# Moving a decoder layer's parameter and weight loads between DMA queues, and a subtraction between engines

## The chip, the cores and the metric

The kernel runs on one core of a Trainium2 chip. TensorE multiplies, VectorE and ScalarE do the arithmetic around it, GpSimd does small element-wise work, and SP issues most of the DMAs. The metric is the device time of one execution in microseconds, given as the median of several runs. A profiled execution leaves a trace, whose span runs from the first to the last instruction.

## What is computed

One layer of a hybrid decoder, for a prompt of 2048 positions and for 8 sample sequences of 4 positions:

```python
xn = _rmsnorm(x, g_attn_norm)
q, k, v, u = split(xn @ w_in)                    # q, k normed per head; 8 heads of 64
branches = [_dilated_branch(q, k, v, r) for r in (1, 4, 16)]   # 128 strided keys each, ALiBi
attn = _merge_branches(branches)                 # weights: softmax over the branches' log-sum-exp
h = x + concat([attn, pool_mixer(u)]) @ w_out
y = h + conv_ffn(_rmsnorm(h, g_ffn_norm))        # up-projection, conv of width 3, SiLU gate, down-projection
```

Each float32 product is made as three products of rounded halves (hi x hi, hi x lo, lo x hi), so every weight and every activation is split first: ScalarE rounds it (line 112), another engine subtracts the rounded part (line 113).

## The kernel before

The work has three stages, each with its own pools in SBUF. The first projects the 16 tiles of 128 rows of the prompt, tile by tile; queries and keys go to DRAM turned and split (`spill_qk`), values as rows (`finish_v`). What belongs to the end of a tile is put off by a number of bursts (`later.after`), and a burst comes at the end of each projection. The last projections are those of the values of tiles 14 and 15, and around them lie the loads for head 0 (`load_qk`, `load_v`): columns 0 to 1535 ahead of them, the last 512 columns behind them, all on SP's queue.

The second stage is attention. It has 192 items, 24 for each of the 8 heads; an item is two blocks of 128 queries of one head and one pattern p (0, 1, 2 for dilation 1, 4, 16). `advance(i)` does the scores of item i, the transposes of item i - 2 and the value products of item i - 3, and copies spread queries on GpSimd for item i + 6 (`spread_next`). From item 8 on the order on every engine is written out by hand (`manual_schedule`, lines 721 to 742); outside it the compiler's scheduler picks the order. Into this loop, at lines 730 to 739, are put:

- the parameter rows of the later stage: `param_load(j)` on SP's queue every 8 items from item 24, turned 13 items later by `param_turn`. Rows and output weights share two buffers (tag `row`);
- the first half (512 columns) of the output weights, one row tile every 5 items from item 150: allocation, load on SP's queue and split, all in one item (lines 735 to 739, tile `rawo`).

The values of the next heads come on SP's queue too (`next_v`, 4 to 8 DMAs each), as do the queries and keys of the next head (`load_head`, 6 DMAs) and the stores of finished outputs (`store_o`).

The third stage merges the three patterns' outputs, multiplies by the output weights (`out_part`, line 817) and runs the feed-forward part. At its start, lines 840 to 846 merge the first four row tiles (`merge`, lines 775 to 797), and load and split the second half of the output weights with `load_rows`: four pairs of row tiles, two of them after the merge of tile 0 and two after that of tile 1, with the subtraction of the split on GpSimd. The loads have three buffers (tag `raw`).

Of the kernel before, what the change touches and what calls it, by code (L numbers as in the profile page):

```python
# [9 lines left out]
F32 = mybir.dt.float32  # L10
# [7 lines left out]
P = 128  # L18
S = 2048
DM = 1024  # L20
KT = DM // P
H = 8
DH = 64
# [8 lines left out]
CH = 512  # L32
# [6 lines left out]
RUN = 4  # L39
# [3 lines left out]
def f32(ap):  # L43
    return ap.bitcast(F32)
# [3 lines left out]
def kernel(ctx, tc, ins, cst, outs):  # L48
    nc = tc.nc
# [8 lines left out]
    w_in0, w_out0, w_up0, w_down0 = w_in[0], w_out[0], w_up[0], w_down[0]  # L58
# [18 lines left out]
    qT_hi = dram.tile([AW, S], F32, name="qT_hi")  # L77
    qT_lo = dram.tile([AW, S], F32, name="qT_lo")
    kT_hi = dram.tile([AW, S], F32, name="kT_hi")
# [31 lines left out]
    def split(hi, lo, src, eng=None):  # L111
        nc.scalar.copy(hi, src)  # L112
        (eng or nc.vector).tensor_tensor(out=lo, in0=src, in1=f32(hi), op=ALU.subtract)  # L113
# [41 lines left out]
    def qk_tile():  # L155
        return pq.tile([P, 3, S], F32R, tag="QK", name="QK", bufs=2)

    def load_qk(h, qk, cols):
        rows = slice(h * DH, (h + 1) * DH)
        Q, KH, KL = (qk[:, i, cols] for i in range(3))  # L160
        nc.sync.dma_start(f32(Q[0:DH]), qT_hi[rows, cols])
        nc.sync.dma_start(f32(Q[DH:P]), qT_lo[rows, cols])
        for half in range(2):
            hr = slice(half * DH, (half + 1) * DH)
            nc.sync.dma_start(f32(KH[hr]), kT_hi[rows, cols])
            nc.sync.dma_start(f32(KL[hr]), kT_lo[rows, cols])

    def bias_table(h):
        tab = pq.tile([P, 3, 2 * P], F32, tag="tab", name="tab", bufs=2)
# [7 lines left out]
        nc.gpsimd.memset(t[:, :, P + 1:P + 2], 1.0)  # L177
        return t

    def load_v(hp, p, t, lo, hi):  # L180

        vs = v_s[:, hp * P:(hp + 1) * P]
        d = t[:, :, 1:P + 1]
        if p == 0:
            nc.sync.dma_start(d, vs.rearrange("(n i) f -> i n f", i=P)[:, lo:hi])
        else:
            r = DILS[p]
            n = min(r, hi - lo)
            for j in range(lo, hi, n):
                J, c = divmod(j, r)  # L190
                src = vs[J * P * r:(J + 1) * P * r].rearrange("(m c i) f -> i m c f", c=r, i=RUN)[:, :, c:c + n]
                for i in range(RUN):
                    nc.sync.dma_start(d[i::RUN, j - lo:j - lo + n, :], src[i])

    rows_of = {}
    stv = state_ffn_conv[0].rearrange("b r c -> (b r) c")
# [1 line left out]
    def param_load(j):  # L198
        n = 2 * NF if j < 4 else 2 * SB
        row = rows_of[j] = p2.tile([2 * NF, 4 * P], F32, tag="row", name="row", bufs=2)  # L200
        if j < 4:
            src = conv_b if j == 3 else conv_w[0, j:j + 1]
            nc.sync.dma_start(row[:, 0:P], src.rearrange("l (c p) -> (l c) p", p=P))
        else:
            nc.sync.dma_start(row[:n], stv[:, (j - 4) * 4 * P:(j - 3) * 4 * P])

    def param_turn(j):
        row = rows_of.pop(j)
# [38 lines left out]

    pair_v, pair_o, heads, spread = {}, {}, {}, {}

    def next_v(hp, p, half):  # L250
        t = value_tile(p2, "V")
        load_v(hp, p, t, 8 * half, 8 * half + 8)
        for b in range(8):
            pair_v[hp, p, 8 * half + b] = t[:, b, :]

# [114 lines left out]
    with tc.tile_pool(name="p1", bufs=1) as p1:  # L370
# [125 lines left out]
        def finish_qk(t, j, ps):  # L496
            rows = P if t >= 0 else NSMP
            a = p1.tile([rows, AW], F32, tag="t", name="a", bufs=4)
            a3 = a.rearrange("p (h d) -> p h d", d=DH)
            nc.scalar.activation(a, ps, AF.Square)  # L500
            ssq = p1.tile([rows, H], F32, tag="ssq", name="ssq", bufs=2)
            nc.vector.tensor_reduce(out=ssq, in_=a3, axis=AX.X, op=ALU.add)
            r = rms_scale(p1, ssq, H, DH)
            nc.vector.tensor_tensor(out=a3, in0=ps.rearrange("p (h d) -> p h d", d=DH),
                                    in1=r[:, :, None].to_broadcast([rows, H, DH]), op=ALU.mult)
            nc.vector.tensor_tensor(out=a, in0=a, in1=g_b[j][:rows], op=ALU.mult)
            if t < 0:
                if j == 0:
                    nc.sync.dma_start(q_smp, a)
                else:  # L510
                    nc.sync.dma_start(nks, a)
                    nc.sync.dma_start(k_smp[:, 3:, :], a)
                return
            if j == 1:
                (nc.gpsimd if t == S // P - 1 else nc.sync).dma_start(nk[t * P:(t + 1) * P, :], a)
            later.after(2, lambda: spill_qk(t, j, a))

        def spill_qk(t, j, a):
            tp = tp4(a)
            for i, dst in enumerate(((qT_hi, qT_lo), (kT_hi, kT_lo))[j]):  # L520
                s = p1.tile([P, 4, P], F32R, tag="qkh", name="qkh", bufs=3)
                d, src = s, tp
                if j == 1:
                    d = s.rearrange("p a (g c i) -> p (a g) c i", c=RES, i=RUN)
                    src = tp.rearrange("p a (g i c) -> p (a g) c i", c=RES, i=RUN)
                if i == 0:
                    hi = d
                    nc.scalar.copy(hi, src)
                else:
                    nc.vector.tensor_tensor(out=d, in0=src, in1=f32(hi), op=ALU.subtract)  # L530
                nc.sync.dma_start(dst.rearrange("(a p) t -> p a t", p=P)[:, :, t * P:(t + 1) * P], f32(s))
# [145 lines left out]
        for half in range(2):  # L677
            pair_o[0, half] = O_first[:, 8 * half:8 * half + 8]
        later.flush()
        load_qk(0, qk, slice(3 * CH, S))  # L680
        load_v(0, 0, v_first[:, 12:16], 12, 16)
        for b in range(16):
            pair_v[0, 0, b] = v_first[:, b, :]
        for i in range(AHEAD):
# [9 lines left out]
    def h_tile(k):  # L694

        return ph.tile([P, 2, TM], F32R, tag=f"h{k}", name="h", bufs=1)
# [13 lines left out]

    with tc.tile_pool(name="p2", bufs=1, reuse_waits="tile") as p2:
        wo0 = [h_tile(k) for k in range(KT)]
        for half in range(2):
            for p in (2, 1):
                next_v(0, p, half)
        nc.vector.memset(stT[:, :, 2 * SB:], 0.0)
        for i in range(AHEAD, AHEAD + SPREAD):
            spread_next(i)
        NEXT_V = {(1, 14): (2, 0), (1, 17): (0, 0), (1, 21): (1, 0), (1, 23): (0, 1), (0, 1): (2, 1), (0, 3): (1, 1)}

        with tc.manual_schedule():
            for i in range(AHEAD, len(items) + 3):
                if i < len(items):
                    h, li = divmod(i, NI)
                    if (i == AHEAD or h and li == 4) and h + 1 < H:
                        load_head(h + 1)

                    if (h % 2, li) in NEXT_V and 0 < h < H - (h % 2):
                        next_v((h + 1) // 2, *NEXT_V[h % 2, li])
                    j, r = divmod(i - NI, 8)  # L730
                    if r == 0 and 0 <= j < 15:
                        param_load(j)
                    if r == 5 and 0 < j < 16:
                        param_turn(j - 1)
                    if i >= 150 and i % 5 == 0 and i < 190:
                        k = ((i - 150) // 5 + 4) % KT
                        raw = p2.tile([P, CH], F32, tag="row", name="rawo", bufs=2)
                        nc.sync.dma_start(raw, wov[:, k, 0:CH])
                        split(wo0[k][:, 0, 0:CH], wo0[k][:, 1, 0:CH], raw)
                    if (h, li) == (7, 0):  # L740
                        mBs[0] = load_pool(0)
                advance(i)
# [3 lines left out]
    with tc.tile_pool(name="p4", bufs=1, reuse_waits="tile") as p4:  # L746
# [11 lines left out]
        def load_rows(view, k0, half, eng=None):  # L758
            raw = raw_tile().rearrange("p (a k) f -> p a (k f)", a=2)
            n = min(2, view.shape[0] // P - k0)  # L760
            nc.sync.dma_start(raw[:, :n], view[k0 * P:(k0 + n) * P, half * CH:(half + 1) * CH]
                              .rearrange("(k p) f -> p k f", p=P))
            w = w_tile().rearrange("p a (b k) f -> p a b (k f)", b=2)
            split(w[:, 0, :n], w[:, 1, :n], raw[:, :n], eng)
            return [w[:, :, i, :] for i in range(n)]
# [4 lines left out]
        def merge_load(t):  # L770
            Om = p4.tile([P, 3, 4, OW], F32, tag="ex", name="om", bufs=2)
            nc.sync.dma_start(Om, o_s.rearrange("(n t) h f -> t n h f", n=3)[t * P:(t + 1) * P])
            return Om
# [63 lines left out]
        NT = S // P  # L837
        res, mAs, ats = {}, {}, {}
        groups = [tuple(range(4))] + [(t, t + 1) for t in range(4, NT, 2)]
        pre = {t: merge_load(t) for t in range(2)}  # L840
        for t in groups[0]:
            ats[t] = merge(pre.pop(t) if t in pre else merge_load(t))
            for k in (((4, 6), (0, 2), (), ()))[t]:
                for j, w in enumerate(load_rows(w_out0, k, 1, nc.gpsimd)):
                    wo[1][k + j] = [w[:, b, :] for b in range(2)]
            res[t] = load_res(t)
        g_ffn_b = p4.tile([P, DM], F32, name="g_ffn_b")
        nc.sync.dma_start(g_ffn_b, g_ffn_norm.to_broadcast([P, DM]))
# [445 lines left out]
```

## Time and profile before

| | |
|---|---|
| median of 3 runs | 2561.21 us (2559.82 to 2563.23) |
| profiled execution | 2559.28 us |
| its span | 2557.5 us |
| TensorE busy | 2486.2 us (97%) |
| VectorE busy | 1725.1 us (67%) |
| ScalarE busy | 1079.1 us (42%) |
| GpSimd busy | 186.6 us (7%) |
| DMA moved | 393.58 MB, 154 GB/s in the mean |

How to read it: a busy TensorE is one with instructions in flight, and its share is an average over stages. The page also cuts the span into 40 slices of 64 us, with the busy tenths of each engine and the TensorE clock that was granted. The rows below are from views of single stretches. PE is TensorE, PEld its weight loads, DVE VectorE, ACT ScalarE, POOL GpSimd, SP the engine that issues DMAs (SPq and POOLq are the issuing queues). L112 is line 112 of the kernel; `out<-in` are the names of the tiles.

### The profile page before, as it was taken

What the parts mean: (1) busy time and instruction counts of PE and PEld (TensorE: products, weight loads), DVE (VectorE), ACT (ScalarE), POOL (GpSimd) and SP (SyncE); (2) the same over time, 40 slices, a digit from 0 to 9 for tenths busy, and PEclk for the clock granted to TensorE, in tenths of its full rate; (3) what the DMA queues carried; (4) which work ended last, traced back from release to release, by engine and by line L of the source; (5) the groups of instructions that cost most, each with busy time, mean ns of one, the idle gap of its engine ahead of it and who ended that gap; (6) DMA issues with size and microseconds to landing.
All of it is one profiled execution on the core that took longest, in us unless ns stands there. A gap on an engine that the chain in (4) does not pass through costs nothing.

```text
span 2557.5 us, 36059 instructions
## 1 busy us (share of the span) xinstructions
PE 2486.2 (97%) x13310; PEld 2119.1 (83%) x13310; DVE 1725.1 (67%) x3819; ACT 1079.1 (42%) x2021; POOL 186.6 (7%) x246
## 2 busy tenths in 40 slices
PE   7999999999968999999999999999999999999999
PEld 5888887999867888788888888888888889999997
DVE  7445344566545785888987789887887666666655
ACT  6333332566544222544333454443444444445442
POOL 1111111333311100000000000000000000000000
PEclk9999999899978999999999999999999999999999
DMA  6333334767644997855558434447443436222321
GB/s 221 106 123 107 128 95 130 183 167 184 155 109 136 312 303 251 258 177 184 170 160 257 124 116 150 127 132 252 144 140 98 137 113 226 84 84 85 92 76 61
DMA packets 412875, 393.58 MB, mean 154 GB/s; under 512 B 16347, under 2 KB 319543, under 8 KB 410012
## 3 DMA queue, kind: packets, MB, share of 16 engines
q1 hardware_dynamic: 412476, 390.48, 50.2%
q8 instruction: 105, 1.72, 0.3%
q0 software_dynamic: 224, 0.80, 0.1%
q14 instruction: 70, 0.57, 0.1%
HBM read 305.70 MB, written 85.52 MB: 153 GB/s over the span
## 4 chain that ended last, share of the span: by engine, by line
PE 66%; DMA 1%; DVE 1%; issue 0%; ACT 0%; SPq 0%; POOL 0%; DVEq 0%; POOLq 0%; ACTq 0%
PE pu L1038 38%; PE pd L1214 19%; PE po L817 5%; PE pd L1208 1%; PE tp L122 0%; DMA raw<-in_w_out_dram 0%; PE Op L325 0%; DMA raw<-in_w_up_dram 0%; PE sacc L990 0%; PE sacc L989 0%; PE po L1071 0%; DVE at L796 0%; PE tpa L802 0%; DMA h_s<-ya 0%; PE tpf L1106 0%
## 5 line engine op out<-in xcount | busy, mean ns | idle before, releaser
L1038 PE MATMUL pu<-h,w 128*128 128x512 f32 (+1 forms) x5232 | 990.6, 350 | 2.1 <-ACT w L112 1.6
L1038 PEld LDWEIGHTS pu<-h,w 128*128 128x128 f32 x5232 | 851.1, 188 | 133.4 <-ACT w L112 2.0
L1214 PE MATMUL pd<-w,act 128*128 128x512 f32 x2112 | 490.2, 392 | 0.0
L1214 PEld LDWEIGHTS pd<-w,act 128*128 128x128 f32 x2112 | 396.6, 188 | 88.1
L112 ACT CAST w<-raw 128x1024 fp32r<-128x1024 f32 (+1 forms) x282 | 287.2, 1027 | 295.6 <-PE pd L1214 171.1
L113 DVE TENSOR_TENSOR w<-raw,w 128x1024 fp32r<-128x1024 f32 (+1 forms) x278 | 328.8, 1186 | 27.1 <-ACT w L112 27.0
L471 PE MATMUL ps<-W_hi,xh 128*128 128x512 f32 x1024 | 332.8, 398 | 1.0 <-ACT xh L112 1.0
L1182 DVE SCALAR_TENSOR_TENSOR cv<-ex,cw,cv 128x512 f32<-128x512 f32 x352 | 262.4, 745 | 29.6 <-ACT cv L1174 27.3
L1172 ACT COPY ex<-pu 128x512 f32<-128x512 f32 (+1 forms) x220 | 110.3, 501 | 346.7 <-PE pu L1038 346.6
L471 PEld LDWEIGHTS ps<-W_hi,xh 128*128 128x128 f32 x1024 | 192.9, 189 | 43.1 <-ACT xh L112 1.5
L296 ACT ACTIVATE Pt<-T,st 128x256 f32<-128x256 f32 (+1 forms) x384 | 157.0, 456 | 130.0 <-DVE st L294 128.0
L325 PE MATMUL Op<-V,PTs 128*128 128x65 f32 x1200 | 168.7, 281 | 37.0 <-ACT PTs L308 28.5
L294 DVE CUSTOM_DVE_ANT_0 T<-Sp,tab 128x256 f32<-128x256 f32 (+1 forms) x384 | 125.0, 364 | 118.0 <-PE Sp L289 78.7
L471 PE MATMUL ps<-W_lo,xh 128*128 128x512 f32 x512 | 202.8, 396 | 0.0
L1216 DVE TENSOR_TENSOR ya<-ya,pd 128x512 f32<-128x512 f32 x192 | 131.0, 684 | 101.6 <-PE pd L1214 101.1
L325 PEld LDWEIGHTS Op<-V,PTs 128*128 128x128 f32 x1200 | 159.7, 203 | 44.8 <-ACT PTs L308 35.3
L95 POOL TENSOR_TENSOR rs<-ms,mhalf 128x8 f32<-128x8 f32 (+3 forms) x68 | 76.5, 1126 | 1585.1 <-DVE stT L1175 1049.5
L1174 ACT ACTIVATE cv<-pu,cw 128x512 f32<-128x512 f32 (+3 forms) x264 | 166.3, 650 | 0.0
L112 ACT CAST act<-cv 128x512 fp32r<-128x512 f32 x88 | 54.6, 620 | 162.5 <-DVE cv L1191 156.3
L471 PEld LDWEIGHTS ps<-W_lo,xh 128*128 128x128 f32 x512 | 96.8, 189 | 19.8
L1175 DVE COPY stT<-ex 128x2 f32<-128x2 f32 x176 | 28.8, 163 | 117.0 <-ACT ex L1172 117.0
L303 PE MATMUL tp<-ident,Pt 128*128 128x128 f32 x600 | 103.8, 286 | 0.0
(225 smaller groups left out, 2739.9 us busy)
## 6 DMA issues: line engine op xcount, KB each, us to landing
raw<-in_w_up_dram SPq DMA_DIRECT2D x176, 512.0 KB
raw<-in_w_down_dram SPq DMA_DIRECT2D x80, 512.0 KB
hn_s<-w SPq DMA_DIRECT2D x16, 1024.0 KB
h<-hn_s SPq DMA_DIRECT2D x32, 512.0 KB
far<-in_cache_k_dram SPq DMA_DIRECT2D x64, 256.0 KB
far<-in_cache_v_dram SPq DMA_DIRECT2D x64, 256.0 KB
om<-o_s SPq DMA_DIRECT2D x16, 792.0 KB
raw<-in_w_in_dram SPq DMA_DIRECT2D x16, 512.0 KB
```

The source lines that it names most:

```text
L112: nc.scalar.copy(hi, src)
L113: (eng or nc.vector).tensor_tensor(out=lo, in0=src, in1=f32(hi), op=ALU.subtract)
L294: nc.vector.tensor_tensor_reduce(out=T[:, :w], in0=Sp[:, s, :w], in1=tab[:, p, 2 * P - w:], op0=ALU.add, op1=ALU.min, scale=1.0, scalar=3e ...
L296: nc.scalar.activation(Pt[:, s, :w], T[:, :w], AF.Exp, bias=st[:, i8:i8 + 1], scale=-1.0)
L325: nc.tensor.matmul(Op[:, i4, :], PT[:, j, :], pair_v[hp, p, b][:, v0:v0 + DH + 1], start=n == 0, stop=n == m - 1)
L471: nc.tensor.matmul(ps, xh[:, a, k, :], (W_hi, W_lo)[b][j, k // 2][:, k % 2, :], start=n == 0, stop=n == 3 * KT - 1)
L817: nc.tensor.matmul(ps, lhs, wo[half][k + 4 * (1 - part)][b], start=part == 0 and k == 0 and i == 0, stop=part == 1 and k == 3 and i == 2)
L1038: nc.tensor.matmul(ps[:, :n], w[:, a, k, :], hs[k][:, b, c0:c0 + n], start=i == 0, stop=i == 3 * KT - 1)
L1174: nc.scalar.activation(d, s, AF.Identity, bias=cw[:, 3, ct:ct + 1], scale=cw[:, 2, ct:ct + 1])
L1182: nc.vector.scalar_tensor_tensor(out=d, in0=e[j], scalar=cw[:, j, ct:ct + 1], in1=d, op0=ALU.mult, op1=ALU.add)
L1214: nc.tensor.matmul(ps, act[0][:, a, k, tau * P:(tau + 1) * P], wd[k][:, b, :], start=k == 0 and j == 0, stop=k == n - 1 and j == 2)
L1216: nc.vector.tensor_tensor(out=ysl, in0=ysl, in1=ps, op=ALU.add)
```

## The change

The diff does five things. The last 512 columns of head 0's queries and keys, and the values with them, are loaded by ScalarE's queue. The first eight value loads of pattern 1 and all 15 parameter rows are loaded by GpSimd's queue. The spill of tile 15's keys is put off by one burst and not two. The first half of the output weights is loaded by GpSimd's queue every 4 items from item 150 on, and the split of a tile stands seven items behind its load. The second half's subtractions go to VectorE, and the loads of its pairs 4 and 6 are asked for ahead of the first merge, those of pairs 0 and 2 behind the merges of tiles 1 and 2.

```diff
-    def load_qk(h, qk, cols):
+    def load_qk(h, qk, cols, eng=None):
+        eng = eng or nc.sync
...
-        nc.sync.dma_start(f32(Q[0:DH]), qT_hi[rows, cols])
+        eng.dma_start(f32(Q[0:DH]), qT_hi[rows, cols])
...
-            nc.sync.dma_start(row[:, 0:P], src.rearrange("l (c p) -> (l c) p", p=P))
+            nc.gpsimd.dma_start(row[:, 0:P], src.rearrange("l (c p) -> (l c) p", p=P))
...
-            later.after(2, lambda: spill_qk(t, j, a))
+            later.after(1 if (t, j) == (S // P - 1, 1) else 2, lambda: spill_qk(t, j, a))
...
-        load_qk(0, qk, slice(3 * CH, S))
-        load_v(0, 0, v_first[:, 12:16], 12, 16)
+        load_qk(0, qk, slice(3 * CH, S), nc.scalar)
+        load_v(0, 0, v_first[:, 12:16], 12, 16, nc.scalar)
...
+        raws = {}
         for half in range(2):
             for p in (2, 1):
-                next_v(0, p, half)
+                next_v(0, p, half, nc.gpsimd if (p, half) == (1, 0) else None)
...
-                    if i >= 150 and i % 5 == 0 and i < 190:
-                        k = ((i - 150) // 5 + 4) % KT
-                        raw = p2.tile([P, CH], F32, tag="row", name="rawo", bufs=2)
-                        nc.sync.dma_start(raw, wov[:, k, 0:CH])
-                        split(wo0[k][:, 0, 0:CH], wo0[k][:, 1, 0:CH], raw)
+                    k, r = divmod(i - 150, 4)
+                    if r == 0 and 0 <= k < KT:
+                        raws[k] = p2.tile([P, CH], F32, tag="row", name="rawo", bufs=2)
+                        nc.gpsimd.dma_start(raws[k], wov[:, (k + 4) % KT, 0:CH])
+                    if r == 3 and 0 < k <= KT:
+                        w = wo0[(k + 3) % KT]
+                        split(w[:, 0, 0:CH], w[:, 1, 0:CH], raws.pop(k - 1))
...
+        def load_second(k):
+            for j, w in enumerate(load_rows(w_out0, k, 1)):
+                wo[1][k + j] = [w[:, b, :] for b in range(2)]
+
         pre = {t: merge_load(t) for t in range(2)}
+        load_second(4)
+        load_second(6)
         for t in groups[0]:
             ats[t] = merge(pre.pop(t) if t in pre else merge_load(t))
-            for k in (((4, 6), (0, 2), (), ()))[t]:
-                for j, w in enumerate(load_rows(w_out0, k, 1, nc.gpsimd)):
-                    wo[1][k + j] = [w[:, b, :] for b in range(2)]
+            if t in (1, 2):
+                load_second(2 * t - 2)
             res[t] = load_res(t)
```

## Rows read from the trace of the kernel before

**Rows 1.** Windows, us: stretch, busy and (instructions) by engine, clock, DMA share, GB/s.
```profile
500.00:690.00 190.00, 186.13 (x1609) 179.82 (x1609) 123.92 (x571) 121.43 (x323) 55.64 (x103) 1.00 0.69 165
699.50:812.30 112.80, 79.74 (x581) 77.33 (x579) 50.46 (x211) 49.26 (x125) 13.09 (x22) 0.77 0.35 94
699.50:724.00 24.50, 0.41 (x4) 0.17 (x2) 2.23 (x10) 1.78 (x5) 0.10 (x1) 0.57 0.77 174
724.00:736.60 12.60, 12.54 (x59) 12.55 (x60) 5.04 (x21) 5.46 (x16) 1.46 (x5) 0.50 0.04 14
788.80:795.00 6.20, 0.61 (x6) 0.37 (x4) 2.00 (x7) 1.48 (x3) 0.00 (x0) 0.71 0.57 161
795.00:802.00 7.00, 6.96 (x34) 6.96 (x35) 2.58 (x12) 2.71 (x8) 0.00 (x0) 0.52 0.14 41
```

**Rows 2.** Waits from 690 us on: waiter, releaser, us in total, times, longest.
```profile
PE Op L325 <- ACT PTs L308: 24.4, 2, 24.1
ACT h L112 <- DMA rawo<-in_w_out_dram: 27.4, 2, 22.6
```

**Rows 3.** Timeline of ScalarE: start, us, line, operation, tiles, [idle before, releaser].
```profile
721.12 0.62 ACT L112 CAST h<-rawo 128x512 fp32r<-128x512 f32 x1 [22.55 <-DMA rawo<-in_w_out_dram]
...
792.36 0.62 ACT L112 CAST h<-rawo 128x512 fp32r<-128x512 f32 x1 [4.82 <-DMA rawo<-in_w_out_dram]
```

**Rows 4.** Timeline of SP's queue, four issues merged.
```profile
707.04 28.93 SPq L738 DMA_DIRECT2D rawo<-in_w_out_dram  x4
```

**Rows 5.** Page, part 5: groups of instructions, busy us, mean ns, idle before.
```profile
L325 PE MATMUL Op<-V,PTs 128*128 128x65 f32 x1200 | 168.7, 281 | 37.0 <-ACT PTs L308 28.5
L303 PE MATMUL tp<-ident,Pt 128*128 128x128 f32 x600 | 103.8, 286 | 0.0
```

**Rows 6.** DMA issues of GpSimd's queue: KB each, us from issue to landing.
```profile
o_s<-O POOLq DMA_DIRECT2D x1, 528.0 KB, 9.3
out_dram<-a POOLq DMA_DIRECT2D x1, 256.0 KB, 9.2
```

**Rows 7.** Timeline of GpSimd: one of these two issues.
```profile
813.45 1.01 POOL L227 DMA_DIRECT2D o_s<-O  x1 [5.24 <-ACT O L329]
```

**Rows 8.** Windows at the head of attention.
```profile
445.40:457.70 12.30, 11.26 (x85) 10.97 (x85) 6.98 (x29) 6.68 (x16) 0.48 (x9) 0.86 0.89 268
457.70:460.00 2.30, 0.05 (x1) 0.08 (x1) 0.00 (x0) 0.00 (x0) 1.33 (x2) 1.00 0.79 198
460.00:480.00 20.00, 19.55 (x94) 19.13 (x94) 7.67 (x41) 7.41 (x21) 6.17 (x7) 0.51 0.66 165
```

**Rows 9.** Timelines at the head of attention: ScalarE, SP's queue, GpSimd.
```profile
448.56 2.46 ACT L296 ACTIVATE Pt<-T,st 128x128 f32<-128x128 f32 x6 [6.75 <-DVE st L294]
...
458.22 15.59 SPq L193 DMA_DIRECT2D V<-v_s  x24
...
458.67 4.13 POOL L241 CAST qs<-QK 128x512 fp32r<-128x512 f32 x4 [6.99 <-DMA QK<-qT_hi]
```

**Rows 10.** Windows at the start of the merge.
```profile
828.10:833.00 4.90, 0.14 (x1) 0.17 (x2) 4.87 (x3) 0.00 (x0) 4.07 (x2) 0.94 0.97 345
833.00:837.50 4.50, 4.50 (x17) 3.71 (x18) 2.89 (x5) 1.75 (x3) 1.91 (x1) 0.69 1.04 413
```

**Rows 11.** Timelines at the start of the merge: VectorE, GpSimd, ScalarE.
```profile
818.23 0.69 DVE L791 TENSOR_TENSOR at<-om,E 128x512 f32<-128x512 f32 x1
...
825.37 1.82 DVE L796 TENSOR_TENSOR at<-at,t 128x512 f32<-128x512 f32 x1
...
830.00 2.71 DVE L796 TENSOR_TENSOR at<-at,t 128x512 f32<-128x512 f32 x1
...
824.26 7.91 POOL L113 TENSOR_TENSOR w<-raw,w 128x1024 fp32r<-128x1024 f32 x3 [9.81 <-DMA ya<-in_x_prompt_dram]
...
834.46 1.05 ACT L112 CAST w<-raw 128x1024 fp32r<-128x1024 f32 x1
```

**Rows 12.** Page, part 5: the split's subtraction on VectorE.
```profile
L113 DVE TENSOR_TENSOR w<-raw,w 128x1024 fp32r<-128x1024 f32 (+1 forms) x278 | 328.8, 1186 | 27.1 <-ACT w L112 27.0
```

More of the change, by code (lines that the diff above doesn't have):

```diff
@@ L156, in qk_tile @@
         return pq.tile([P, 3, S], F32R, tag="QK", name="QK", bufs=2)
-    def load_qk(h, qk, cols):
+    def load_qk(h, qk, cols, eng=None):
+        eng = eng or nc.sync
         rows = slice(h * DH, (h + 1) * DH)
         Q, KH, KL = (qk[:, i, cols] for i in range(3))
-        nc.sync.dma_start(f32(Q[0:DH]), qT_hi[rows, cols])
-        nc.sync.dma_start(f32(Q[DH:P]), qT_lo[rows, cols])
+        eng.dma_start(f32(Q[0:DH]), qT_hi[rows, cols])
+        eng.dma_start(f32(Q[DH:P]), qT_lo[rows, cols])
         for half in range(2):
             hr = slice(half * DH, (half + 1) * DH)
-            nc.sync.dma_start(f32(KH[hr]), kT_hi[rows, cols])
-            nc.sync.dma_start(f32(KL[hr]), kT_lo[rows, cols])
+            eng.dma_start(f32(KH[hr]), kT_hi[rows, cols])
+            eng.dma_start(f32(KL[hr]), kT_lo[rows, cols])
     def bias_table(h):
@@ L178, in value_tile, with load_v @@
         return t
-    def load_v(hp, p, t, lo, hi):
+    def load_v(hp, p, t, lo, hi, eng=None):
+        eng = eng or nc.sync
         vs = v_s[:, hp * P:(hp + 1) * P]
@@ L184, in load_v @@
         if p == 0:
-            nc.sync.dma_start(d, vs.rearrange("(n i) f -> i n f", i=P)[:, lo:hi])
+            eng.dma_start(d, vs.rearrange("(n i) f -> i n f", i=P)[:, lo:hi])
         else:
@@ L192, in load_v @@
                 for i in range(RUN):
-                    nc.sync.dma_start(d[i::RUN, j - lo:j - lo + n, :], src[i])
+                    eng.dma_start(d[i::RUN, j - lo:j - lo + n, :], src[i])
     rows_of = {}
@@ L202, in param_load @@
             src = conv_b if j == 3 else conv_w[0, j:j + 1]
-            nc.sync.dma_start(row[:, 0:P], src.rearrange("l (c p) -> (l c) p", p=P))
+            nc.gpsimd.dma_start(row[:, 0:P], src.rearrange("l (c p) -> (l c) p", p=P))
         else:
-            nc.sync.dma_start(row[:n], stv[:, (j - 4) * 4 * P:(j - 3) * 4 * P])
+            nc.gpsimd.dma_start(row[:n], stv[:, (j - 4) * 4 * P:(j - 3) * 4 * P])
     def param_turn(j):
@@ L248, with next_v @@
     pair_v, pair_o, heads, spread = {}, {}, {}, {}
-    def next_v(hp, p, half):
+    def next_v(hp, p, half, eng=None):
         t = value_tile(p2, "V")
-        load_v(hp, p, t, 8 * half, 8 * half + 8)
+        load_v(hp, p, t, 8 * half, 8 * half + 8, eng)
         for b in range(8):
```

## The prediction

> **What bounds the kernel now.** Read the page's 40 slices first: TensorE is busy in nine tenths of nearly every slice, with a hole near 700 us and a thinner stretch up to about 840 us. So a change to queues can only pay where TensorE stands still, and the stretches there come next.
>
> The windows [rows 1] show it. Between 500 and 690 us, the undisturbed middle of attention, 1609 TensorE instructions take 190 us, which is 8.47 a us with the granted clock at 1.00 (2.4 GHz). From 699.5 to the end of attention at 812.3 us there are 581, worth 581 / 8.47 = 68.6 us at that pace, but they take 112.8 us: 44.2 us are lost. The waits [rows 2] give the cause. TensorE waits once for 24.1 us on the transposed scores that ScalarE copies, and ScalarE itself waits 27.4 us in two waits, the longest 22.6 us, for `rawo`, the rows of the output weights. ScalarE's timeline [rows 3] places them: the first split at 721.12 us and the last at 792.36 us. The SP queue [rows 4] says why the data is late: the first four `rawo` issues take it from 707.04 us to 736.0 us, and the first of them starts 7.5 us after TensorE had already stopped, since head 7's loads and the value loads stand ahead of it. The last one ends another wait of 4.82 us. In lines 735 to 739 the load and the split that needs it stand in the same item, so every delay of the queue goes straight into ScalarE, and from there into TensorE.
>
> **Pace of an item.** Two groups of the page [rows 5] have 1200 value matmuls and 600 transposes over 192 items; with 4 score matmuls each (lines 288 and 289) that is 6.25 + 3.13 + 4 = 13.4 instructions, or 13.4 / 8.47 = 1.58 us an item.
>
> **The change part by part.**
> Output weights, first half (the main term). The load goes to GpSimd's queue and its split comes seven items later (load at i = 150 + 4k, split at i = 157 + 4k): 7 x 1.58 = 11.1 us. The issue costs GpSimd about 1.0 us [rows 7], so about 10.0 us are left for the transfer. Its price is not in the trace for this load; the two loads and stores that GpSimd's queue already issues land after 9.2 and 9.3 us [rows 6], both in stretches like those where the DMA engines are 0.89 to 0.97 busy [rows 8, 10]. I take 9.2 us, as it has the same 256 KB, and count the waits as gone. Worth, from [rows 1], each stretch less its instructions at 8.47 a us: 699.5 to 724 us 24.5 - 0.5 = 24.0; the stretch behind it, where the clock was granted at 0.50 (1.2 GHz) after TensorE had stood still, 12.6 - 7.0 = 5.6; 788.8 to 795 us 6.2 - 0.7 = 5.5; the slow stretch behind that 7.0 - 4.0 = 3.0. Sum **38.1 us**. The other 44.2 - 38.1 = 6.1 us I leave: there are still eight splits, each with the same two instructions on ScalarE and VectorE, and they may bring back the small gaps. The bounds: 44.2 us if those go too; 19 us, rival 1, if transfers stay late.
>
> New waits in it: load k may only start when split k - 2 has freed one of two buffers, one item earlier. Queued behind it on GpSimd are the spread queries, issued six items ahead (9.5 us), and nobody waits. Cost 0. Parameter rows: 15 issues of about 1.0 us go from SP to GpSimd, which is busy 55.64 of 190 us in the middle [rows 1]; the row's release is three items old by then. Cost 0, gain 0, since TensorE's pace there has no hole for SP's queue to fill. If GpSimd were late, the spread queries would hold TensorE by about 1 us for each issue.
>
> The output weights' second half, lines 840 to 846 (`merge` and `load_rows`). After 828.1 us TensorE stands 4.9 us and then runs 4.5 us at clock 0.69 [rows 10]. In that time GpSimd does three subtractions in 7.91 us, and VectorE's merge instructions, which TensorE waits for, take up to 2.71 us [rows 11] where the same kind took 0.69 us before GpSimd began. VectorE does the subtraction in 1186 ns [rows 12]. Off GpSimd, the merge of tile 1 is 3 x 0.69 + 2 x 1.19 = 4.4 us from 825.4 us on, so done at about 829.8 us and not at 832.7: 2.9 us earlier. The four subtractions add 4 x 1.19 = 4.7 us to VectorE, which has room under the projection matmuls. The fourth pair of rows waits for one of three buffers and is cast only at 834.46 us [rows 11], so TensorE may wait there next. Bounds 0 and 6.1 us (all of the gap and 1.2 us of the slow clock); I take **3 us**.
>
> The Trainium skill, SBUF — State Buffer, section "SBUF: two separate sides" (its box on the trap that VectorE blocks a transfer), speaks against the first term: a load from GpSimd's queue can be held while VectorE has the port that the two share, 620 ns becoming 3100 ns. By it the 9.2 us would be an estimated 11.7 us, over the 10.0 that are left, and the sum would end near rival 3. [Rows 6] are two such transfers, and neither shows it.
>
> Head 0's last loads. Seven issues go to ScalarE, at about 0.65 us each by the 24 value loads in 15.59 us [rows 9]: 4.6 us, into ScalarE's idle time ahead of 448.56 us (6.75 us). But four of them wait for the key store of tile 15 and one for its values, and behind them on ScalarE stand the first exponentials; until now SP carried that wait. The earlier spill (one burst, not two) should bring the key store ahead of the value stores on SP. Eight value loads go to GpSimd, ahead of the spread queries: at about 1.0 us each [rows 7] from 451.7 us, where GpSimd now starts to idle for 6.99 us, they end near 459.7 us, and the queries began at 458.67 us [rows 9]. Gain: the 2.3 us gap at 457.7 us and, with it, the slow stretch behind. From 445.4 to 480 us there are 180 instructions, worth 21.3 of 34.6 us, so at most 13.3 us [rows 8]. Loss: if the exponentials wait for tile 15's values, whose load SP issued just before 458.22 us [rows 9], ScalarE starts up to about 9 us late. I take **0**, since the queries start near 459 us either way, and keep a gain of 13 and a loss of 9.
>
> Sum: 38.1 + 3 + 0 = **41.1 us**. The profiled execution's span of 2557.5 us becomes 2516.4; its own time 2559.28 (1.78 over the span) becomes 2518.2. The median shown is 2561.21, 1.9 above it: **2520 us**.
>
> **Rivals.**
> 1. The transfers are late wherever they are issued. In 699.5 to 724 us the DMA engines were 0.77 busy [rows 1]; if the first `rawo` still lands only with head 7's loads near 721 us, ScalarE, which wants it about five items on, at 699.5 + 5 x 1.58 = 707.4 us, still waits 13.6 us, and the slow stretch of 5.6 us stays: 2520 + 19 = 2539 us. For it: the load. Against: the new queue doesn't stand behind SP's issues. Chance 0.12. The Trainium skill says the same in DMA: Bandwidth & Descriptors, "Issuing engines are not separate DMA queues": another engine saves the issue time, not the transfer.
> 2. ScalarE is held at the head of attention as described, 9 us and some slow clock: 2531 us. Chance 0.13. For it: the wait for the stores is real; against: the scheduler may put the exponentials first.
> 3. Slower: loads on GpSimd's queue land so late that all eight splits wait. Each wait stops ScalarE, hence TensorE, and brings a slow stretch of 3.0 us as after 795 us. Eight times (x + 3.0) eats 41 us at x = 2.1 us, so it decides from a landing of 10.0 + 2.1 = 12.1 us; at 13 us the kernel takes 2520 + 8 x 6 = 2568 us. Against: 9.2 us was taken under full load, and the engines are far emptier after 724 us. Chance 0.06.
> 4. The head of attention gains as well, about 11 us: 2508 us. Chance 0.10.
> 5. It doesn't do what it says: the waits stay since the items' order ends up as before: 2561 us. Chance 0.03; the items' order is written by hand.
>
> **How the numbers follow.** Forecast 0.56, at 2512 to 2529 us (3 us of the second half either way, and about 6 us of the small gaps or of the head of attention). The range 2507 to 2540 takes in rivals 1, 2 and 4 and leaves 0.09 out, beside edges. A measurement of this kernel can tell about 0.2% (5 us) from no change. Faster: 0.56 + 0.12 + 0.13 + 0.10 = 0.91; within: 0.03; slower: 0.06.
>
> **What would show it.** Right: no wait of ScalarE on `rawo` over 1 us, 581 instructions in about 75 us with the clock at 1.00, and attention ending near 774 us. GpSimd shows about 31 more issues. The merge's VectorE instructions stay at 0.69 us and TensorE's gap at its start is under 3 us. Wrong: a wait of ScalarE ahead of the first exponentials longer than 6.75 us (rival 2), casts of `rawo` that end a wait on DMA (rivals 1 and 3; one or eight tell them apart), or TensorE waiting on spread queries or on head 7's loads, which no row shows now.

## The result and the profile after

| | before | changed |
|---|---|---|
| median on one chip | 2562.22 us (2559.82 to 2567.02) | 2520.88 us (2519.39 to 2523.36) |
| ratio | | 0.9837 (95% interval 0.982 to 0.9854) |
| profiled execution | 2559.28 us | 2523.36 us |
| its span | 2557.5 us | 2521.3 us |
| TensorE busy | 2486.2 us | 2472.2 us |
| mean granted clock | 0.983 | 0.994 |

The change saves 41.3 us by the medians, against 41.1 us forecast. The forecast of 2520 us was right to 1 us, but not each of its terms: two that were wrong cancel, as the experiments show. Between the two profiled executions the saving is 36.2 us, so some 5 us of the 41.3 stand in no trace; single executions of the kernel before ran from 2553.66 to 2569.41 us over the comparisons of this text.

The first view is the windows of the changed kernel (stretch, then busy time and instructions of TensorE, its weight loads, VectorE, ScalarE, GpSimd; granted clock, DMA share, GB/s):

```profile
500.00:690.00 190.00, 186.14 (x1612) 179.95 (x1611) 124.30 (x569) 122.07 (x323) 62.77 (x121) 1.00 0.69 165
695.70:773.20 77.50, 71.38 (x581) 68.27 (x579) 48.92 (x209) 48.47 (x125) 16.58 (x29) 0.96 0.51 138
743.00:752.20 9.20, 9.07 (x52) 8.83 (x52) 4.85 (x23) 4.64 (x12) 2.38 (x4) 0.63 0.21 48
```

The undisturbed middle is as fast as before (1612 instructions in 190 us, 1609 in [rows 1]), though GpSimd has 18 instructions more in it. The last 581 instructions of attention took 112.8 us [rows 1] and now take 77.5: 35.3 us are gained, and 8.9 of the 44.2 lost ones stay.

The tile `rawo` tells why (duration of an instruction in ns: min, median, max; then the first and last start in us):

```profile
L742 POOL DMA_DIRECT2D rawo<-in_w_out_dram x8: 536/536/620, 693.0 to 742.3; - x8
L112 ACT CAST h<-rawo x8: 614/617/624, 705.6 to 756.5; 128x512 fp32r<-128x512 f32 x8
...
DMA to landing us min/median/max: 2.8/5.0/10.7
```

The loads are issued from 693.0 us on, where SP came to the first at 707.04 us [rows 4]. None of ScalarE's waits in the stretch is for `rawo`; in [rows 2] they were 27.4 us. From the issue of a load to its cast there are 11.3 to 18.8 us (12.7 for the first, issued at 692.96 us and cast at 705.61), more than the longest landing of 10.7 us.

**Where the rest went.** Five markers cut the span into pieces that every kernel has: the load of the bias table for head 0, the first turn of a parameter row (item 37), the 45 projection products behind the last value product, the first product with the second half of the output weights, and the first down-projection. Timelines of SP and TensorE, the kernel before:

```profile
428.25 0.38 SPq L668 DMA_DIRECT2D base<-const_dram  x1
513.30 0.25 PE L212 MATMUL tpc<-ident,row 44*128 44x44 f32 x1
812.27 10.75 PE L817 MATMUL po<-h,act 128*128 128x512 f32 x45
833.60 4.05 PE L817 MATMUL po<-w,act 128*128 128x512 f32 x12
1078.84 3.41 PE L1214 MATMUL pd<-w,act 128*128 128x512 f32 x14
```

and the changed one:

```profile
431.30 0.38 SPq L670 DMA_DIRECT2D base<-const_dram  x1
509.75 0.25 PE L214 MATMUL tpc<-ident,row 44*128 44x44 f32 x1
773.24 10.66 PE L823 MATMUL po<-h,act 128*128 128x512 f32 x45
795.52 3.30 PE L823 MATMUL po<-w,act 128*128 128x512 f32 x12
1042.63 7.59 PE L1226 MATMUL pd<-w,act 128*128 128x512 f32 x32
```

The differences of these times, for all kernels of this text (the third stage is 833.60 - 812.27 = 21.33 and 1078.84 - 833.60 = 245.24, so 266.6 us for the kernel before):

| kernel | to the bias table | head of attention | rest of attention | third stage to the down-projection |
|---|---|---|---|---|
| before | 428.3 | 85.0 | 299.0 | 266.6 |
| changed | 431.3 | 78.4 | 263.5 | 269.4 |
| changed, profiled again (f1) | 428.6 | 78.9 | 260.8 | 270.4 |
| e1, split later, SP's queue | 431.8 | 85.7 | 278.9 | 266.8 |
| e2, GpSimd's queue only | 430.0 | 84.7 | 277.2 | 267.9 |
| e3, output weights' first half alone | 428.9 | 84.5 | 261.2 | 267.3 |
| e4, head put back | 430.3 | 86.3 | 260.9 | 272.0 |
| e5, second half put back | 431.5 | 78.5 | 263.6 | 266.1 |
| e6, parameter rows put back | 428.5 | 79.1 | 261.1 | 269.6 |
| f2, spill put back | 430.4 | 90.6 | 262.5 | 270.4 |
| f3, value loads put back | 430.2 | 95.0 | 260.9 | 271.5 |
| f4, new order in the third stage | 430.4 | 79.5 | 260.9 | 263.5 |
| g1, key stores on GpSimd | 430.1 | 88.8 | 261.0 | 271.5 |
| g2, f4 and g1 together | 428.6 | 89.1 | 260.9 | 263.9 |

What follows the last marker is 1478.6 to 1480.0 us in all of them. The first column moves by 3.5 us between executions with no regard to the change (431.3 and 428.6 us for the same changed kernel). So of the saving, 35.5 us stand in the rest of attention, 6.6 us in the head, and the third stage lost 2.8 us.

### The profile page after: what moved, and what is told of

The parts are those of the page before. It is cut to its first block, busy times and chain, and to the rows that moved or that the text cites. A ratio compares the mean times of both kernels' runs of the same rounds, so it can differ in the third digit from the quotient of the medians.

```text
span 2521.3 us, 36064 instructions
## 1 busy us (share of the span) xinstructions
PE 2472.2 (98%) x13310; PEld 2102.8 (83%) x13310; DVE 1720.4 (68%) x3823; ACT 1078.1 (43%) x2021; POOL 193.4 (8%) x273
## 4 chain that ended last, share of the span: by engine, by line
PE 63%; DMA 1%; DVE 1%; issue 0%; ACT 0%; POOL 0%; SPq 0%; POOLq 0%
PE pu L1050 39%; PE pd L1226 19%; PE po L823 2%; PE pd L1220 1%; DMA om<-o_s 1%; PE sacc L1002 0%; PE sacc L1001 0%; PE po L1083 0%; DMA raw<-in_w_up_dram 0%; PE tp L122 0%; PE tpf L1118 0%; DVE xn L108 0%; DVE t L797 0%; PE tps L961 0%; DVE w L113 0%
## 5 line engine op out<-in xcount | busy, mean ns | idle before, releaser
L327 PE MATMUL Op<-V,PTs 128*128 128x65 f32 x1200 | 160.5, 271 | 10.6 <-DVE PTs L308 5.4
L327 PEld LDWEIGHTS Op<-V,PTs 128*128 128x128 f32 x1200 | 150.4, 193 | 19.3 <-ACT PTs L310 11.7
```

The lines of the kernel that those rows point to most:

```text
L327: nc.tensor.matmul(Op[:, i4, :], PT[:, j, :], pair_v[hp, p, b][:, v0:v0 + DH + 1], start=n == 0, stop=n == m - 1)
```

## Experiments

The theory: the first half's gain needs both the other queue and the distance between load and split, and is nearly all of the result; the head nets some 6 us, by a chain of edits; the second half's move loses, by the order in which VectorE then works. Each median stands beside that of the kernel before on the same chip.

**Queue or distance (e1, e2, e3).** e1 is the kernel before with the new loop of the change (a load every 4 items and not every 5, its split seven items later), but

```diff
-                        nc.gpsimd.dma_start(raws[k], wov[:, (k + 4) % KT, 0:CH])
+                        nc.sync.dma_start(raws[k], wov[:, (k + 4) % KT, 0:CH])
```

> The kernel before with one edit: the loads of the output weights' first half stay on SP's queue, but the split of each comes seven items behind its load (and every 4 items, as in the changed kernel). Theory D (the distance between load and split is what pays): no wait of ScalarE on rawo over 1 us, and about 36 to 38 us under the kernel before, 2524 to 2526 us. Rival Q (the queue is what pays, since SP is late with the first issue): the first rawo is issued near 707 us again, lands 5 to 9 us later or more, while its split stands near 709 us, so ScalarE waits once for 5 to 12 us with a slow stretch of 3 to 6 us behind it; the gain is 20 to 30 us, 2532 to 2542 us.

Measured: 2544.4 us beside 2559.95, ratio 0.9936 (0.9919 to 0.9953). SP's queue, ScalarE and TensorE:

```profile
711.20 15.86 SPq L739 DMA_DIRECT2D rawo<-in_w_out_dram  x3
725.36 0.62 ACT L112 CAST h<-rawo 128x512 fp32r<-128x512 f32 x1 [11.80 <-DMA rawo<-in_w_out_dram]
728.05 1.97 PE L325 MATMUL Op<-V,PTs 128*128 128x65 f32 x8 [12.67 <-DVE PTs L306]
727.00:743.00 16.00, 14.95 (x75) 14.96 (x76) 7.09 (x34) 7.91 (x19) 2.63 (x3) 0.53 0.11 34
```

One wait is left, that for the first tile, 14.2 us after its issue. TensorE stands 12.7 us, and 727 to 743 us run at a granted clock of 0.53. The distance alone brings 20.1 of the 37.8 us that e3 brings below in the rest of attention: rival Q's mechanism. By the medians it is 15.6 us, less than the 20 to 30 expected of Q.

e2 is the kernel before with one word changed:

```diff
-                        nc.sync.dma_start(raw, wov[:, k, 0:CH])
+                        nc.gpsimd.dma_start(raw, wov[:, k, 0:CH])
```

> The kernel before with one edit: the loads of the output weights' first half are issued by GpSimd's queue, with load and split in the same item as before. Rival Q: the queue alone brings most of the gain, 2522 to 2530 us. Theory D: each split waits for its own landing (median 5.0 us in the changed kernel) less the 1.5 us by which GpSimd runs ahead of ScalarE, 3 to 4 us, eight times; with a slow stretch of up to 3 us behind each wait that costs 28 to 56 us against the changed kernel, so 2549 to 2577 us, from a little under the kernel before to above it.

Measured: 2536.86 us beside 2559.95, ratio 0.9905 (0.9888 to 0.9923). Tile and timelines:

```profile
DMA to landing us min/median/max: 2.8/3.0/10.8
698.01 0.62 POOL L738 DMA_DIRECT2D rawo<-in_w_out_dram  x1
703.87 0.62 ACT L112 CAST h<-rawo 128x512 fp32r<-128x512 f32 x1 [4.00 <-DMA rawo<-in_w_out_dram]
706.80 1.12 PE L325 MATMUL Op<-V,PTs 128*128 128x65 f32 x4 [5.58 <-ACT PTs L308]
707.17 0.54 POOL L738 DMA_DIRECT2D rawo<-in_w_out_dram  x1 [0.32 <-issue]
717.96 0.62 ACT L112 CAST h<-rawo 128x512 fp32r<-128x512 f32 x1 [1.22 <-DMA rawo<-in_w_out_dram]
```

Neither expectation holds. Not eight splits wait but two (5.2 us in all): the median landing is 3.0 us, and the other six casts come 5.3 to 11.1 us behind the issues of their loads. Yet the first wait of 4.0 us makes TensorE stand 5.6 us, with slow stretches behind it. So the queue alone brings 21.8 us there, the distance alone 20.1. Each takes away most of the long wait; only both take away the last one, and with it the slow clock.

e3 is the kernel before with both, and nothing else of the change.

> The kernel before with the output weights' first half alone changed: load on GpSimd's queue and split seven items later. As predicted: 38 us, 2523 us. As the segments of the runs so far read (35 to 38 us between the first turn of parameter rows and the last value product): 2523 to 2526 us. If the parameter rows on GpSimd's queue had a share in that stretch: less, 2528 us or more.

Measured: 2525.34 us beside 2560.65, ratio 0.9865 (0.9844 to 0.9886): 35.3 us by the medians, 37.8 us in the rest of attention by the markers. This is the main term, and it needs no other part of the change.

**The head of attention (e4, f2, f3, g1).** e4 is the changed kernel with the loads of the head on SP's queue and the spill two bursts later:

```diff
-            later.after(1 if (t, j) == (S // P - 1, 1) else 2, lambda: spill_qk(t, j, a))
+            later.after(2, lambda: spill_qk(t, j, a))
...
-        load_qk(0, qk, slice(3 * CH, S), nc.scalar)
-        load_v(0, 0, v_first[:, 12:16], 12, 16, nc.scalar)
+        load_qk(0, qk, slice(3 * CH, S))
+        load_v(0, 0, v_first[:, 12:16], 12, 16)
...
-                next_v(0, p, half, nc.gpsimd if (p, half) == (1, 0) else None)
+                next_v(0, p, half)
```

> The changed kernel with the head of attention put back: head 0's last loads and the first value loads on SP's queue, the spill of tile 15's keys two bursts later. As predicted (the head nets 0): 2521 us, within 2 us of the changed kernel. As the markers of the two traces read (from the load of the bias table to the first turn of parameter rows the changed kernel took 6.7 us less): 2527 to 2528 us, the gap at 457 us and the stretch at clock 0.50 behind it are back, and the start 3 us later in the projection stage, which the edit does not touch, stays or goes by chance.

Measured: 2528.33 us beside 2559.95, ratio 0.9868 (0.9849 to 0.9886). The head takes 86.3 us and not 78.4, as the markers had it, but not by the mechanism that was expected. The gap is back; the long stretch at clock 0.50 behind it is not. TensorE comes to the keys of head 1 at 488 us instead, and waits for them 6.4 us in all:

```profile
461.02 0.47 PE L290 MATMUL Sp<-QK 128*128 128x256 f32 x2 [1.99 <-DMA QK<-kT_hi]
465.00:487.00 22.00, 21.51 (x188) 21.04 (x187) 14.18 (x69) 14.28 (x41) 7.97 (x12) 0.98 0.69 164
492.08 0.44 PE L290 MATMUL Sp<-QK 128*128 128x128 f32 x1 [4.00 <-DMA QK<-kT_hi]
494.88 0.45 PE L291 MATMUL Sp<-QK 128*128 128x128 f32 x1 [2.36 <-DMA QK<-kT_lo]
```

In the kernel before, e1, e2 and e3 the stretch at 0.50 behind the gap lasts some 20 us, and no wait for head 1's keys follows. So the old head loses at one of two places, and about as much at either. The five kernels with the old head take 84.5 to 86.3 us, the five with the whole new head 78.4 to 79.5.

f2 puts back only the spill (the first of these hunks), f3 only the last one.

> The changed kernel with one edit: the spill of tile 15's keys comes two bursts later again, all else of the head as changed. Theory A (the early store on SP stands between the loads that the first scores need, 434.9 to 445.1 us, and costs the 5 us by which the first scores come later): scores start near 446.7 us and the kernel takes 2515 to 2518 us. Rival B (the store was brought forward since ScalarE's loads of the last keys wait for it, with the exponentials behind them): ScalarE's queue is held until the store near 448 us has landed, the first exponentials start at 454 us or later, as late as now, and the kernel takes 2520 to 2525 us.

> The changed kernel with one edit: the first eight value loads of pattern 1 back on SP's queue, ahead of the other 16. If the head's gain of 7 us comes from the last keys on ScalarE's queue alone (the gap at 457 to 460 us was a wait for them): 2521 us, no change. If it comes from the value loads leaving SP: SP's 16 loads of 11.7 us become 24 of 16.8 us, head 1's queries and keys come 5 us later, and up to 5 to 7 us return: 2526 to 2528 us.

Measured beside 2561.43 us: f2 2534.72 us, ratio 0.9892 (0.9873 to 0.9911); f3 2534.31 us, ratio 0.9886 (0.9867 to 0.9905); the changed kernel in the same comparison (f1) 2519.79 us, ratio 0.9831 (0.9811 to 0.9851).

> The changed kernel as it is, as the measure for the three runs beside it: 2519 to 2523 us, with 78 to 79 us from the load of the bias table to the first turn of parameter rows, 262 to 265 us from there to the last value product of attention, 21.5 to 23 us to the first product with the second half of the output weights, and 1725 to 1728 us to the end.

Putting back either edit costs some 15 us, twice what the whole head brings, so no expectation had the size. TensorE in f2 (first two lines) and in f3, with the window behind f3's waits:

```profile
463.53 0.65 PE L290 MATMUL Sp<-QK 128*128 128x256 f32 x2 [4.16 <-DMA QK<-kT_hi]
466.75 0.55 PE L291 MATMUL Sp<-QK 128*128 128x256 f32 x1 [2.15 <-DMA QK<-kT_lo]
...
494.12 0.45 PE L290 MATMUL Sp<-QK 128*128 128x128 f32 x1 [3.97 <-DMA QK<-kT_hi]
497.02 0.45 PE L291 MATMUL Sp<-QK 128*128 128x128 f32 x1 [2.45 <-DMA QK<-kT_lo]
497.00:517.00 20.00, 19.98 (x95) 20.00 (x96) 6.95 (x33) 7.48 (x20) 2.16 (x2) 0.50 0.62 129
```

In f2 the last keys of head 0 come late, in f3 the keys of head 1, which stand behind 24 value loads on SP instead of 16, as in e4. In f3 the wait of 6.4 us is the smaller part: the 20 us behind it at clock 0.50 do 95 instructions, worth 95 / 8.47 = 11.2 us, so 8.8 us are lost there.

g1 asks whether the head's late start (first scores 20.5 us after the bias table, 17.2 before) can be had back. In the changed kernel, SP issues tile 15's key stores at 438.43 us, between head 0's first and second load; g1 gives them to GpSimd:

```diff
-                nc.sync.dma_start(dst.rearrange("(a p) t -> p a t", p=P)[:, :, t * P:(t + 1) * P], f32(s))
+                (nc.gpsimd if (t, j) == (S // P - 1, 1) else nc.sync).dma_start(
+                    dst.rearrange("(a p) t -> p a t", p=P)[:, :, t * P:(t + 1) * P], f32(s))
```

> The changed kernel with one edit: the stores of tile 15's keys are issued by GpSimd and not by SP, still one burst after the projection. If the 4 us by which the first scores come later (20.4 us and not 16.4 us behind the load of the bias table) are SP's, whose six loads for head 0 stand behind those two stores: the scores start 16 to 17 us behind that load, the last keys land as early as now, and the kernel takes 2514 to 2516 us. Rival: the DMA engines are full there (1.0 busy), so the loads land no earlier, or GpSimd issues the stores late behind the bias tables and the last keys come late again as in the run with the spill put back: 2520 to 2534 us.

Measured: 2532.16 us beside 2560.65, ratio 0.9885 (0.9863 to 0.9906). The scores start 18.6 us after the bias table, 1.9 us earlier, and the kernel loses. The time lies in the rival's range, but not for its reason: TensorE waits for no keys behind the first scores. ScalarE in g1, and below it in the changed kernel:

```profile
457.78 0.91 ACT L298 ACTIVATE Pt<-T,st 128x256 f32<-128x256 f32 x2
463.40 0.39 ACTq L187 DMA_DIRECT2D V<-v_s  x1
463.89 0.91 ACT L298 ACTIVATE Pt<-T,st 128x256 f32<-128x256 f32 x2 [5.21 <-issue]
...
462.15 0.91 ACT L298 ACTIVATE Pt<-T,st 128x256 f32<-128x256 f32 x2
463.08 0.39 ACTq L187 DMA_DIRECT2D V<-v_s  x1
463.58 0.91 ACT L298 ACTIVATE Pt<-T,st 128x256 f32<-128x256 f32 x2 [0.52 <-DVE st L296]
```

In both, the load of tile 15's values can go only at about 463 us, when their store is done; SP's own value loads start within 0.1 us of it, at 463.16 and 463.45 us. In g1 ScalarE comes to it at 458.7 us and stands there with the exponentials queued behind; in the changed kernel it comes as the load is free to go. In f2 ScalarE stands 5.6 us at the same load. This is the prediction's second rival: the mechanism is real, and as these traces read, only the late start hides it in the changed kernel. A kernel with that one load on another queue was not tried.

**The second half of the output weights (e5, f4, g2).** e5 is the changed kernel with the old lines of this part (GpSimd's subtraction, pairs behind merges).

> The changed kernel with the output weights' second half put back: subtractions on GpSimd, pairs 4 and 6 behind the merge of tile 0, pairs 0 and 2 behind that of tile 1. As predicted (the move brings 3 us): 2524 us, with TensorE standing 4.8 us ahead of the second transposes of the merge. As the trace of the changed kernel reads (VectorE's new order holds the low half of tile 0's merge by 3.6 us; 1 to 3 us lost from the end of attention to the end of the kernel): 2518 to 2520 us.

Measured: 2518.22 us beside 2559.95, ratio 0.9831 (0.9811 to 0.9851). By the medians that is not told apart from the changed kernel; by the markers the third stage takes 266.1 us, the same as in the four other kernels with the old lines (266.6 to 267.9), against 269.4 to 272.0 in the seven with the changed ones. The means are 267.0 and 270.7 us, so the move costs 3.7 us. VectorE in the changed kernel, then TensorE and a window:

```profile
786.42 0.68 DVE L797 TENSOR_TENSOR at<-om,E 128x512 f32<-128x512 f32 x1
787.02 0.68 DVE L797 TENSOR_TENSOR t<-om,E 128x512 f32<-128x512 f32 x1
787.62 1.22 DVE L113 TENSOR_TENSOR w<-raw,w 128x1024 fp32r<-128x1024 f32 x1
788.76 0.69 DVE L802 TENSOR_TENSOR at<-at,t 128x512 f32<-128x512 f32 x1
789.36 0.69 DVE L113 TENSOR_TENSOR ml<-tpa,mh 128x512 fp32r<-128x512 f32 x1
790.10 0.80 PE L823 MATMUL po<-h,ml 128*128 128x512 f32 x1 [3.58 <-DVE ml L113]
790.00:795.00 5.00, 4.90 (x13) 3.87 (x14) 3.69 (x11) 1.16 (x2) 0.00 (x0) 0.50 0.97 328
```

The merge's instructions stay at 0.69 us, as forecast: the contention with GpSimd is gone (2.71 us in [rows 11], and 2.71 us again in e5, where GpSimd subtracts). But VectorE now does the weights' subtractions and the merge of tile 1 ahead of `ml`, the low half of tile 0's merge. TensorE stands for it 3.6 us, and runs slow behind it. This takes the place of the 4.8 us ahead of the second transposes, and up to the first product with the second half nothing is won or lost: 22.2 us in the mean of either group. The 3.7 us are lost behind it, where the old lines take 243.7 to 246.1 us to the down-projection and the changed ones 247.1 to 249.6. There (855 to 935 us) TensorE stands 3.2 us for the next tiles' halves and norms, 0.3 us in e5, in an order that the scheduler made anew; which instruction of VectorE holds them was not tested.

f4 keeps the subtraction on VectorE and asks for things in another order:

```diff
-        load_second(4)
-        load_second(6)
         for t in groups[0]:
             ats[t] = merge(pre.pop(t) if t in pre else merge_load(t))
-            if t in (1, 2):
-                load_second(2 * t - 2)
+            if t == 0:
+                mAs[0] = merge_t(ats.pop(0))
+            if t == 1:
+                load_second(4)
+                load_second(6)
+                load_second(0)
+            if t == 2:
+                load_second(2)
```

> The changed kernel with the start of the third stage in another order: the transposed merge of tile 0 is asked for right after its merge, and pairs 4, 6 and 0 of the output weights behind the merge of tile 1, pair 2 behind that of tile 2, with the subtractions on VectorE as changed. If the 3.6 us wait for the low half of tile 0's merge is what eats the move's gain: that wait goes, 19 us and not 22.3 us from the last value product to the first product with the second half, and if the later waits of the stage (3 us between 855 and 935 us) come from the old order too, they go as well: 2515 to 2518 us. Rival: VectorE does the subtractions ahead of tile 1's merge anyway, so TensorE waits for that: within 1 us of 2521 us.

Measured: 2516.34 us beside 2561.43, ratio 0.9821 (0.9801 to 0.9842), against 2519.79 for f1. VectorE and TensorE:

```profile
782.55 0.69 DVE L113 TENSOR_TENSOR ml<-tpa,mh 128x512 fp32r<-128x512 f32 x1
783.30 0.50 PE L823 MATMUL po<-h,ml 128*128 128x512 f32 x1
787.54 0.63 PE L808 MATMUL tpa<-ident,at 128*128 128x128 f32 x4 [1.67 <-DVE at L802]
```

As expected, `ml` comes in time, the second transposes wait 1.7 us (4.8 in the kernel before), and the stage takes 263.5 us: 3.1 less than in the kernel before, 6.9 less than in f1. Against f1 both pieces gain: 18.7 us and not 22.3 up to the first product with the second half, 244.8 and not 248.1 behind it. The subtractions are on VectorE in both kernels, so it was the order that cost, not their work; f4 moves the transposed merge and the loads together, and which of the two does it is open. It has the lowest median of all kernels here, 3.5 us under f1; the intervals of the two overlap, so it is the markers that set them apart.

g2 is f4 and g1 together.

> The two edits together: tile 15's key stores on GpSimd's queue, and the new order at the start of the third stage. If they add: 3.5 to 7 us from the second and 4 us from the first, 2510 to 2514 us. If the first brings nothing: 2516 us.

Measured: 2524.76 us beside 2560.65, ratio 0.9858 (0.9838 to 0.9877). The third stage keeps f4's 263.9 us, the head has 89.1 like g1 (88.8): the parts add, with their signs, and the time is above both expectations since g1's sign was the other one.

**Parameter rows (e6).** The changed kernel with `nc.sync` for the two loads in `param_load`.

> The changed kernel with the 15 parameter rows back on SP's queue. As predicted (they cost and bring nothing): 2518 to 2523 us, the stretch from the first turn of parameter rows to the last value product 261 to 264 us. Rival: SP's queue is near its limit in attention, as the value loads put back on it showed at the head, and the rows delay a head's queries and keys: one or more waits of TensorE on QK of 2 to 4 us, each with a slow stretch, 2525 to 2535 us.

Measured: 2520.47 us beside 2560.65, ratio 0.9843 (0.9826 to 0.9861), and the same pieces as f1 to 1 us. The rows cost and bring nothing.

## Why the prediction was right, and where it was not

- **The stretch and its pace** (8.47 instructions a us, 44.2 us lost): right. Only the 28.93 us of SP's first four issues [rows 4] were misread as the queue's work: they go at 707.04, 707.72, 722.49 and 735.64 us, an issue takes 0.35 us, and between them SP stands for the two buffers. The 581 instructions now take 77.5 us, where 68.6 + 6.1 = 74.7 were expected; f1, without the slow stretch at 743 us, has 2.7 us less in this piece of the table.
- **Output weights, first half, 38.1 us**: right in mechanism and size; alone it gave 35.3 us by the medians and 37.8 by the markers. Its inputs were rough: a landing of 9.2 us was taken, they ran from 2.8 to 10.7 with a median of 5.0 (up to 11.9 in e3); an issue of 1.0 us was taken, it took 0.54. The longest landing was past the 10.0 us that were left; that ScalarE waited for none is due to the distance, at least 11.3 us and 12.7 for the first load where 11.1 was forecast. That casts of `rawo` would be late anyway (rival 1) or eight times (rival 3) did not show. Of what the Trainium skill says in SBUF — State Buffer, "SBUF: two separate sides", no run here shows a sign: the median landing is under half of the 11.7 us worked out by it, and the longest one in e2, 10.8 us, is shorter than SP's at the same time (next point).
- **Rival 1's premise**, a transfer that is late whoever issues it: true in part. In the kernel before, the first cast comes 14.1 us behind SP's issue at 707.04 us [rows 3, 4]; in e2 the second comes 10.8 us behind GpSimd's issue at 707.17 us. What the other queue saves is first of all the place of the issue: e2's first load goes at 698.01 us, 9.0 us earlier than SP's, and its cast starts at 703.87 us and not at 721.12. So far the traces agree with the rule quoted from the Trainium skill, DMA: Bandwidth & Descriptors, "Issuing engines are not separate DMA queues". The 3.3 us between the two landings go beyond it; they are one pair with other transfers ahead of them, so how much of them is the queue is open.
- **Parameter rows, 0**: right (e6).
- **Second half, +3**: wrong in sign, -3.7. The step that failed was to count VectorE's 4.7 us of subtractions as lying in free room. The room was there in the sum, but not in front of `ml`: a wait of 3.6 us took the place of the one of 4.8 us, and VectorE's new order lost the 3.7 us behind it. In f4 the order was another, and the third stage gained 3.1 us.
- **Head, 0**: wrong, about +6.4. The trade was read on the right rows ([rows 8, 9]) but not weighed: a late start costs 3.3 us once, while the 2.3 us gap that it removes carried a stretch at clock 0.50 with it. The forecast also took the eight value loads only as a delay for the spread queries. These began at 463.87 us and not near 459, and no wait of TensorE for them stands in the trace; but head 1's keys, which stand behind the value loads on SP, were not looked at, and e4 and f3 wait 6.4 us for them. Rival 4 had the sign, and 11 us were too many.
- **Rival 2**: not what happened, but f2 and g1 show it to be close (ScalarE stands 5.6 and 5.2 us).

The terms make 35.48 + 6.60 - 2.82 = 39.26 us between the profiled executions, less 3.05 us of the first column: 36.2, the difference of the spans (2521.3 us, where 2516.4 was forecast). That the median met the forecast to 1 us is in part luck: the head's missed gain and the second half's missed loss nearly cancel, and the 5 us by which the medians differ more than the profiled executions make up for what the terms fall short.

## What to carry to other kernels

A load that an engine waits for in the order written by hand needs both: a queue on which nothing slow stands ahead of it, and a distance to its use that is longer than its longest landing. Price a wait of TensorE together with the stretch at the lower clock behind it, since in f3 and g1 the stretch cost more than the wait. Work given to an engine with free time still has a place in that engine's order: look at which instruction it comes ahead of.

## What the runs showed that was not expected

- One of two linked edits can be worse than none: the head's edits gain 6.4 us together, but without the earlier spill, or without the value loads on GpSimd, the head takes 90.6 and 95.0 us, against 85.0 in the kernel before.
- Starting earlier can lose: in g1 the first scores come 1.9 us sooner, and the head takes 10 us more, because ScalarE reaches a DMA issue before its data is there.
- The stretch at a granted clock of 0.50 (1.2 GHz) behind a stop of TensorE is not in proportion to the stop: 12.6 us behind 24.1 us [rows 1, 2], but 22 us (465 to 487 us) behind 4.4 us in g1, and some 3 us (462 to 466 us) behind 2.5 us in e4.
- The same projection stage ended 428.3 to 431.8 us into the span, kernel by kernel, though no edit stands ahead of its last tile.
